# Seven block products in all four feed-forwards of a two-layer flow-matching trunk

## The chip, the cores and the metric

One core of one Trainium2 chip runs the whole program. The metric is device time in microseconds (us), from the launch to the end of the program; lower is better. Engines are called TensorE (PE in the profile, PEld its weight loads), VectorE (DVE), ScalarE (ACT), GpSimd (POOL) and SyncE (SP, which issues the loads).

## The reference, cut to what matters

```python
def swiglu(h, w_gu, w_down):
    g, u = jnp.split(h @ w_gu, 2, axis=-1)
    return (jax.nn.silu(g) * u) @ w_down

def run_layer(x, cond, lp, rope, ctx):
    mod = (jax.nn.silu(cond) @ lp['w_mod'] + lp['b_mod']).reshape(cond.shape[0], N_MOD, 1, D_MODEL)
    nw = lp['norm_w']
    h = rmsnorm(x, nw[0]) * (1 + mod[:, 1]) + mod[:, 0]
    x = x + 0.5 * mod[:, 2] * swiglu(h, lp['ffn1_wgu'], lp['ffn1_wd'])
    h = rmsnorm(x, nw[1]) * (1 + mod[:, 4]) + mod[:, 3]
    out, new_ctx = token_mix(h, lp, rope, ctx)
    x = x + mod[:, 5] * out
    h = rmsnorm(x, nw[2]) * (1 + mod[:, 7]) + mod[:, 6]
    x = x + 0.5 * mod[:, 8] * swiglu(h, lp['ffn2_wgu'], lp['ffn2_wd'])
    return x, new_ctx
```

Two layers; 128 context and 512 latent tokens; model width 1024; feed-forward width 2816; all in float32. The nine modulation vectors of a layer are nine times eight columns of 128, each a product of two conditioning vectors with a 1024 by 128 block of `w_mod`.

## The kernel before, in words

Activations stand transposed: 8 tiles of 128 features by 640 tokens, in two halves of 320 tokens (`HO = (1, 0)`; half p = 1 goes first, half q = 0 holds the context tokens and so has two segments). Every matrix product is made of three matmuls for each 128 by 128 weight block: weight and activation are each split into a rounded part and a remainder (`wh`, `wl` and `xh`, `xl`), and the three leading products are added up in PSUM. A weight tile of four blocks (128 x 512) is loaded (`w`), copied rounded by ScalarE (`wh`, line 162) and subtracted by VectorE (`wl`, line 171). There are 7 buffers each of `wh` and `wl`, and 3 of `w`.

A feed-forward has 22 blocks f of 128 hidden features. The plain one, `ffn` (line 427), makes for each block and token half 8 x 2 x 3 = 48 matmuls for gate and up, in two halves of 11 blocks, each followed by its part of the down product. `ffn7` (line 483) is used for the last feed-forward alone. It makes 2 blocks plainly (`PLAIN`), and from there each block by seven products of quarter size instead of eight: P1, P2, Q3 to Q7, each 4 x 3 = 12 matmuls, so 84 a block instead of 96. For that, sums of weight quarters are needed (four additions of 128 x 512 on GpSimd a block, `load` and `r1`), sums of activation quarters (once, `sums7` on GpSimd and `split7`), and the results are put together by nine VectorE operations of 128 x 320 a block. Blocks go in chunks of 4, each chunk followed by its down product, 16 groups of 12 matmuls.

In `ffn7` the order is written out by hand: `order` is the list of TensorE's groups, and `put(t, ...)` hangs every other operation on a place t in it. Up to the last chunk everything is kept in program order on its engine (`s.pin`). Each weight tile is split a few places before its group: 5 for most, 3 for Q4.

The modulation columns of later steps are made on VectorE by two multiplications with a running sum, of 128 x 1024 each (`mod_cols`, line 321), from a 512 KB load on SyncE's queue. `mod_steps` (line 348) hands them out along the plain feed-forwards: 56 columns beside the first one of layer 0, 24 and 48 beside the next two (`MOD2`, `STEPS1` to `STEPS3`). The last feed-forward has none. `norm_half` (line 398) and `norm7_half` (line 471) make the normalised input of a half as soon as the half's last sum of squares is there; the last `TAIL` = 2 outputs of the feed-forward before are done half p first, so that p's normalisation can go on beside q's rest.

Of the kernel before, what the change touches and what calls it, by code (L numbers as in the profile page):

```python
# [47 lines left out]
def spread(n, a, b):  # L48

    return lambda i: (min(max(i + 1 - a, 0), b - a) * n) // (b - a) - (min(max(i - a, 0), b - a) * n) // (b - a)  # L50

MOD2 = 3

STEPS1, STEPS2, STEPS3 = (4, 66), (10, 66), (4, 66)

HEAD, TAIL, TAIL_O = 2, 2, 3
# [7 lines left out]
PLAIN, K2 = 2, KT // 2  # L66
# [38 lines left out]
class Trunk:  # L105
# [168 lines left out]
    def start(s, mc):  # L274
# [16 lines left out]
        s.h = [s.H() for _ in range(KT)]  # L291
        bm, nw = mc["sp"][:, S_OFF["bmod"][0]:S_OFF["bmod"][1]], mc["sp"][:, S_OFF["nw"][0]:S_OFF["nw"][1]]
        for f0 in range(0, KT, 4):
            fs = slice(f0, f0 + 4)
            for j in (1, 0):
# [6 lines left out]
                row = s.slots.alloc(512, False, "B")  # L302
# [13 lines left out]
            for h in HO:  # L316
                for f in range(f0, f0 + 4):
                    s.norm_tile(0, h, f, rs[h])

    def mod_cols(s, mc, j, f, pin=False):  # L320

        nc = s.nc
        l, m = mc["l"], mc["m"]
        cs = s.cs
        q = j * KT + f
        w = s.wm[q % 2]
        nc.sync.dma_start(out=w, in_=s.a["wmod"][l, q])
# [20 lines left out]
    def mod_steps(s, n):  # L348

        for _ in range(n):  # L350
            if s.todo:
                mc, j, f = s.todo.pop(0)
                s.mod_cols(mc, j, f, True)
                if f == KT - 1:
                    s.mod_fin(mc, j)
# [71 lines left out]
    def ffn(s, wgu, wd, i, mods, done):  # L427

        step = 0
        for hf in range(2):  # L430
            acts = [s.A(2 * T, True) for _ in range(NH)]
            w = {} if hf else {0: s.ahead}
            for mi, h in s.halves(NH, 0 if hf else HEAD, 0):
                m = hf * NH + mi
                if mi not in w:
                    w[mi] = [s.prep(wgu[m, n], KT) for n in range(2)]
                wg, wu = w[mi]
                av = acts[mi].v(2, r=True)
                sl = s.hs(h)
                g = s.proj(wg, h)  # L440
                u = s.proj(wu, h, ps=s.bank())
                t = s.norm.tile([P, H], F32, name="th", tag="tmp", bufs=4)
                s.act(t, g[:, :H], AF.Tanh, scale=0.5)
                s.stt(t, t, 1.0, g[:, :H], ALU.add, ALU.mult)
                s.tt(t, t, u[:, :H], ALU.mult)
                s.split(av[:, 0, sl], av[:, 1, sl], t)
                s.mod_steps(mods(step))
                step += 1
            if hf == 1:
                s.free(s.h)  # L450
            w = {}
            for o, h in s.halves(KT, 0, TAIL if hf else 0):
                if o not in w:
                    w[o] = s.prep(wd[o][:, hf * NH:hf * NH + NH, :], NH)
                sl = s.hs(h)
                ps = s.bank() if (2 * o + h) % 2 else s.wbank()
                s.mms(ps[:, :H], w[o], s.hl_of(acts, sl), NH)
                s.x_update(ps, i, o, h)
                if hf == 1:
                    done(o, h)  # L460
                s.mod_steps(mods(step))
                step += 1
            for a in acts:
                a.free()
# [5 lines left out]


    def norm7_half(s, i, h):

        p, q = HO
        if h == p:
            s.h = [s.H() for _ in range(KT)]
            s.xf = [s.slots.alloc(2 * H, False, "B").v(2) for _ in range(K2)]
        else:
            reg = [s.A(4 * H).v(2, 2) for _ in range(K2 // 2)]
            s.xq = [reg[k // 2][:, k % 2] for k in range(K2)]  # L480
        ps = s.bank()
        s.mm(ps[:, :H], s.ones, s.ss[h])
        r = s.norm_r(ps)
        for k in range(KT):
            t = s.norm_tile(i, h, k, r)
            f = (s.xf if h == p else s.xq)[k % K2][:, k // K2]
            for c, a, b in s.segs(h):
                o = slice(a - h * H, b - h * H)
                s.act(f[:, o], t[:, o], AF.Identity, bias=s.mB[:, c, i, k:k + 1])
# [31 lines left out]
    def ffn7(s, wgu, wd, i, mods, done):  # L521
        p, q = HO
        step = [0]

        def beside():
            s.mod_steps(mods(step[0]))
            step[0] += 1


        sums = [s.A(4 * H, True).v(2, 2, r=True) for _ in range(3 * K2 // 2)]  # L530
        s.s7 = [[sums[(3 * k + j) // 2][:, (3 * k + j) % 2] for j in range(3)] for k in range(K2)]
        acts = [s.A(2 * T, True) for _ in range(PLAIN)]
        w = {0: s.ahead}
        n = 0
        for mi, h in s.halves(PLAIN, PLAIN, 0):
            if mi not in w:
                w[mi] = [s.prep(wgu[mi, e], KT) for e in range(2)]
            g = s.proj(w[mi][0], h)
            u = s.proj(w[mi][1], h, ps=s.bank())
            av, sl = acts[mi].v(2, r=True), s.hs(h)  # L540
            t = s.norm.tile([P, H], F32, name="th", tag="tmp", bufs=4)
            s.act(t, g[:, :H], AF.Tanh, scale=0.5)
            s.stt(t, t, 1.0, g[:, :H], ALU.add, ALU.mult)
            s.tt(t, t, u[:, :H], ALU.mult)
            s.split(av[:, 0, sl], av[:, 1, sl], t)
            if h == q:
                s.sums7(n)
                n += 1
            beside()
        w = {}  # L550
        per = WK // PLAIN
        for o in range(KT):
            if o % per == 0:
                r, (wh, wl) = s.raw(), s.hilo()
                for e in range(per):
                    s.nc.sync.dma_start(out=r[:, e * PLAIN:e * PLAIN + PLAIN, :], in_=wd[o + e][:, :PLAIN, :])
                s.split(wh, wl, r)
            for h in (q, p):
                ps = s.bank() if (2 * o + h) % 2 else s.wbank()
                xs = s.hl_of(acts, s.hs(h))  # L560
                for k in range(PLAIN):
                    e = o % per * PLAIN + k
                    s.three(ps[:, :H], (wh[:, e, :], wl[:, e, :]), xs(k), k == 0, k == PLAIN - 1)
                s.x_update(ps, i, o, h)
                beside()
            if o < K2:
                if n < K2:
                    s.sums7(n)
                    n += 1
# [7 lines left out]
        order, chunks = [], []
        m = PLAIN
        while m < NM:
            chunks.append(range(m, min(m + WK, NM)))  # L580
            m += WK
        tails = set()
        for ci, ch in enumerate(chunks):
            for f in ch:
                new = [(f, n) for n in ("P1", "Q5", "P2", "Q6", "Q3", "Q7")]
                if f > PLAIN:
                    done3 = f == ch[0]
                    new = [x for x in new if not (done3 and x[1] in ("P1", "Q5", "P2"))]
                    if not done3:
                        new.insert(1, (f - 1, "Q4"))  # L590
                order += new
# [3 lines left out]
            if ci + 1 < len(chunks):  # L595
                g = f + 1
                order += [(g, "P1"), (f, "Q4"), (g, "Q5"), (g, "P2")]
# [26 lines left out]
        def tile(f, n, src):  # L624

            def fn():
                ws[f, n] = s.hilo()
                s.split(*ws[f, n], src())
            return fn

        for f in range(PLAIN, NM):
# [36 lines left out]
            put(Q7 + 2, lambda d=d, f=f: s.stt(d["q"], d["q"], 1.0, prods[f, "c"], ALU.add, ALU.mult))  # L668
            put(Q7 + 2, lambda d=d: s.stt(d["q"], d["q"], -1.0, d["t5"], ALU.mult, ALU.mult))
# [6 lines left out]
            put(Q7 + 3, lambda d=d, f=f: s.act(out(f, q)[:, 0], d["q"]))  # L676
            put(Q7 + 4, lambda d=d, f=f: s.tt(out(f, q)[:, 1], d["q"], out(f, q)[:, 0].bitcast(F32), ALU.subtract))
# [1082 lines left out]
```

## Time and profile before

| | us |
|---|---|
| median of 3 runs | 3153.7 (3150.43 to 3154.25) |
| the profiled execution's own time | 3150.53 |
| its span, first to last instruction | 3148.7 |
| TensorE busy | 3087.9 |
| VectorE busy | 2136.4 |
| ScalarE busy | 1220.8 |
| GpSimd busy | 140.0 |

Busy time is the time in which an engine had at least one of its instructions under way. Instructions of one engine overlap in the profile at their ends, so what a series of them takes is read from start to start. A window of the profile is a stretch in us from the span's start. The feed-forwards lie at about 56 to 533, 1142 to 1611, 1612 to 2090 and 2708 to 3149 us; the rest is the start and the two mixers.

### The profile page before, as it was taken

To read this page: it belongs to the slowest core of one execution; us is meant where nothing else is said; L and a number is where in the kernel's file an instruction comes from. 1 tells how busy PE (TensorE), PEld (TensorE's weight loads), DVE (VectorE), ACT (ScalarE), POOL (GpSimd) and SP (SyncE) were. 2 spreads that over 40 slices of the span, in tenths; PEclk is the share of its full clock that TensorE was granted. 3 is DMA by queue.
4 is the path that set the end of the run, shared out by engine and by line. 5 is a ranking of instruction groups with operands and counts; after the bars stand their busy time and mean duration, and the time that the engine had idled before them with its cause. 6 is when DMAs were issued, how large, how long until landed. Compare 5 with 4: busy or idle time off the path is not lost.

```text
span 3148.7 us, 54263 instructions
## 1 busy us (share of the span) xinstructions
PE 3087.9 (98%) x21206; PEld 2929.5 (93%) x21206; DVE 2136.4 (68%) x4268; ACT 1220.8 (39%) x2444; POOL 140.0 (4%) x118
## 2 busy tenths in 40 slices
PE   8999999999999999999999999999999999899999
PEld 5999998998887999999999999989989779799999
DVE  5667677757758774555566666676685687887776
ACT  4222223346544442222242223243464454444443
POOL 0000000000000000000000000000000000232221
PEclk9999999999999999999999999999999999999999
DMA  6445452454322422332323443434533224122222
GB/s 221 135 142 172 140 162 88 138 159 121 120 71 72 142 82 91 115 117 98 115 77 131 148 147 129 146 102 130 167 111 97 65 73 143 54 84 81 83 82 81
DMA packets 261468, 364.87 MB, mean 116 GB/s; under 512 B 97708, under 2 KB 143612, under 8 KB 260476
## 3 DMA queue, kind: packets, MB, share of 16 engines
q1 hardware_dynamic: 252572, 340.66, 34.1%
q10 hardware_dynamic: 8640, 20.76, 1.8%
q8 instruction: 166, 2.72, 0.4%
q14 instruction: 90, 0.74, 0.1%
HBM read 325.37 MB, written 35.96 MB: 115 GB/s over the span
## 4 chain that ended last, share of the span: by engine, by line
PE 89%; DVE 6%; ACT 3%; DMA 1%; issue 1%; SPq 0%; POOL 0%; DVEq 0%; ACTq 0%; POOLq 0%
PE wacc L188 47%; PE acc L188 42%; DVE tn L179 1%; ACT t_A L162 1%; DVE wl L171 1%; DVE t_H L179 1%; DVE t_S L1291 1%; DVE t_A L171 1%; ACT t_H L162 1%; ACT t_B L162 0%; DVE t_A L179 0%; ACT t_W L162 0%; DVE t L179 0%; ACT wh L162 0%; DMA w<-in_wd 0%
## 5 line engine op out<-in xcount | busy, mean ns | idle before, releaser
L188 PE MATMUL wacc<-t_H,wh 128*128 128x320 f32 x5248 | 1188.3, 312 | 24.5 <-ACT t_H L162 9.4
L188 PEld LDWEIGHTS wacc<-t_H,wh 128*128 128x128 f32 x5248 | 877.9, 187 | 52.5 <-DVE t_H L179 14.3
L188 PE MATMUL wacc<-t_H,wl 128*128 128x320 f32 x2624 | 812.3, 311 | 2.5 <-DVE wl L171 2.5
L162 ACT ACTIVATE wh<-w 128x512 fp32r<-128x512 f32 (+2 forms) x772 | 470.4, 613 | 746.5 <-PE wacc L188 488.3
L171 DVE TENSOR_TENSOR wl<-w,wh 128x512 fp32r<-128x512 f32 (+2 forms) x772 | 528.4, 686 | 251.0 <-ACT wh L162 245.1
L188 PE MATMUL acc<-t_H,wh 128*128 128x320 f32 x2496 | 556.6, 308 | 0.0
L188 PE MATMUL acc<-t_A,wh 128*128 128x320 f32 x2272 | 503.6, 308 | 0.2 <-DVE t_A L171 0.2
L188 PEld LDWEIGHTS wacc<-t_H,wl 128*128 128x128 f32 x2624 | 491.5, 187 | 10.3 <-issue 5.3
L188 PE MATMUL wacc<-t_A,wh 128*128 128x320 f32 x2048 | 468.2, 310 | 9.3 <-DVE tg L179 5.5
L188 PEld LDWEIGHTS acc<-t_H,wh 128*128 128x128 f32 x2496 | 418.5, 188 | 0.8 <-ACT wh L162 0.2
L188 PE MATMUL acc<-t_H,wl 128*128 128x320 f32 x1248 | 383.6, 308 | 0.0
L188 PEld LDWEIGHTS acc<-t_A,wh 128*128 128x128 f32 x2272 | 380.1, 188 | 0.8 <-DVE t_A L171 0.5
L188 PEld LDWEIGHTS wacc<-t_A,wh 128*128 128x128 f32 x2048 | 345.2, 188 | 17.3 <-DVE tg L179 6.6
L188 PE MATMUL acc<-t_A,wl 128*128 128x320 f32 x1136 | 350.0, 308 | 0.3 <-DVE wl L171 0.3
L188 PE MATMUL wacc<-t_A,wl 128*128 128x320 f32 x1024 | 317.3, 310 | 2.0 <-DVE wl L171 2.0
L188 PEld LDWEIGHTS acc<-t_H,wl 128*128 128x128 f32 x1248 | 234.0, 188 | 0.1
L188 PEld LDWEIGHTS acc<-t_A,wl 128*128 128x128 f32 x1136 | 213.3, 188 | 0.5 <-DVE wl L171 0.5
L179 DVE SCALAR_TENSOR_TENSOR t_A<-acc,mG,t_A 128x320 f32<-128x320 f32 (+1 forms) x192 | 88.4, 479 | 178.8 <-PE acc L188 173.7
L188 PEld LDWEIGHTS wacc<-t_A,wl 128*128 128x128 f32 x1024 | 192.5, 188 | 5.2 <-DVE wl L171 2.2
L171 DVE TENSOR_TENSOR th<-th,acc 128x320 f32<-128x320 f32 x136 | 66.0, 487 | 186.9 <-PE acc L188 186.9
L162 ACT ACTIVATE t_A<-th 128x320 fp32r<-128x320 f32 x176 | 82.7, 471 | 248.4 <-DVE th L171 221.6
L179 DVE SCALAR_TENSOR_TENSOR t_W<-t_W 128x1024 f32<-128x1024 f32 x128 | 156.3, 1221 | 2.1
(201 smaller groups left out, 3086.0 us busy)
## 6 DMA issues: line engine op xcount, KB each, us to landing
w<-in_wgu SPq DMA_DIRECT2D x292, 256.0 KB, 2.8
t_W<-in_wmod SPq DMA_DIRECT2D x128, 512.0 KB, 4.1
w<-in_win SPq DMA_DIRECT2D x168, 256.0 KB, 3.0
w<-in_wd SPq DMA_DIRECT2D x136, 256.0 KB, 2.8
gd<-tg SPq DMA_DIRECT2D x96, 160.0 KB, 2.2
tg<-gd SPq DMA_DIRECT2D x96, 160.0 KB, 2.3
t_B<-in_wgu SPq DMA_DIRECT2D x40, 256.0 KB, 2.8
w<-in_wd SPq DMA_DIRECT2D x48, 192.0 KB, 2.4
```

The lines of the kernel that those rows point to most:

```text
L162: return s.order(s.nc.scalar.activation(out=out, in_=in_, func=func, **kw))
L171: return s.order(s.nc.vector.tensor_tensor(out=out, in0=a, in1=b, op=op))
L179: return s.order(s.nc.vector.scalar_tensor_tensor(out=out, in0=a, scalar=sc, in1=b, op0=op0, op1=op1, **kw))
L188: return s.order(s.nc.tensor.matmul(out, lhsT, rhs, start=start, stop=stop, **kw))
L1291: nc.vector.tensor_reduce(out=nm2.ap[:, i:i + 1], in_=ps[:, :H], axis=AX.X, op=ALU.max)
```

## The change

All four feed-forwards go through `ffn7`, with four settings (`CHUNKS`): the sizes of the chunks, how many blocks after the first chunk are still plain (`then`), and how many modulation columns go with each step of the first chunk's gate and up, and of its down product. The first chunk is plain: 6 blocks, then 2 more, in the first feed-forwards of both layers (8 plain, 14 by seven products), and 3 blocks in the second ones (3 plain, 19 by seven products). `MOD2` goes from 3 to 4, so 32 columns belong to the second feed-forward and 40 to the third. Columns left over after the first chunk are spread evenly over the places of `order`. The seven products of a block come in the order P1, Q5, Q6, P2, Q7, Q3 (Q4 after the next block's P1), and what reads PSUM at a place is put ahead of the modulation, and both ahead of the splits of weights. In the normalisation the extra copies of half p are done later (`later`), and half q is copied first and split from the copy. `ffn` and the separate schedule of columns go.

```diff
-MOD2 = 3
-STEPS1, STEPS2, STEPS3 = (4, 66), (10, 66), (4, 66)
-HEAD, TAIL, TAIL_O = 2, 2, 3
+MOD2 = 4
+TAIL, TAIL_O = 2, 3
-PLAIN, K2 = 2, KT // 2
+CHUNKS = (((6, 4, 4, 4, 4), 2, 1, 0.5), ((3, 4, 4, 4, 3, 4), 0, 0, 0.25), ((6, 4, 4, 4, 4), 2, 1, 0.5), ((3, 4, 4, 4, 3, 4), 0, 0, 0))
+K2 = KT // 2
...
+    def mod_next(s, n):
+        s.owed += n
+        while s.owed >= 1 and s.todo:
+            s.owed -= 1
+            mc, j, f = s.todo.pop(0)
+            load, a, b = s.mod_cols(mc, j, f)
+            load()
+            s.pin = True
+            a()
+            s.pin = False
+            b()
...
+    def norm7_tile(s, i, h, k, r):
+        x, hv = s.x[k], s.h[k].v(2, r=True)[:, :, s.hs(h)]
+        if h == HO[0]:
+            t = s.xf[k % K2][:, k // K2]
+            A, B = s.mA[:, 1, i, k:k + 1], s.mB[:, 1, i, k:k + 1]
+            s.stt(t, x[:, s.hs(h)], A, r, ALU.mult, ALU.mult)
+            s.act(hv[:, 0], t, AF.Identity, bias=B)
+            s.stt(hv[:, 1], t, B, hv[:, 0].bitcast(F32), ALU.add, ALU.subtract)
+            s.later.append(lambda: s.act(t, t, AF.Identity, bias=B))
+            return
...
+        s.split(hv[:, 0], hv[:, 1], t)
...
+        acts[0] = s.A(2 * T, True)
+        todo = [s.later[:K2], s.later[K2:]] + [[lambda k=k: s.sums7(k)] for k in range(K2)]
+        if not then:
+            sums()
+            todo += [[lambda k=k: s.split7(k)] for k in range(K2)]
+        s.first = True
 
         def beside():
-            s.mod_steps(mods(step[0]))
-            step[0] += 1
...
+            if not s.first:
+                s.mod_next(mods)
+            s.first = False
+            if todo:
+                for fn in todo.pop(0):
+                    fn()
+        eight(0, n0, beside)
+        w0 = {}
         for o in range(KT):
...
+            w0[o] = s.prep(wd[o][:, :n0, :], n0)
             for h in (q, p):
                 ps = s.bank() if (2 * o + h) % 2 else s.wbank()
...
+                s.mms(ps[:, :H], w0[o], s.hl_of([acts[f] for f in range(n0)], s.hs(h)), n0)
                 s.x_update(ps, i, o, h)
...
+                s.mod_next(dmods)
...
+        if then:
+            sums()
+            todo += [[lambda k=k: s.split7(k)] for k in range(K2)]
+            eight(n0, then, lambda: [fn() for fn in todo.pop(0)])
+        rest()
...
+        n, end = len(s.todo), min(tails) - 8
+        for e, (mc, j, f) in enumerate(s.todo):
+            t = e * end // n
+            for fn, d in zip(s.mod_cols(mc, j, f), (0, 4, 5)):
+                put(t + d, fn, late=1)
...
-            s.ffn(s.a["wgu1"][l], s.a["wd1"][l], 0, spread(len(s.todo), *(STEPS3 if l else STEPS1)), s.normed(1, s.ahead_mix(l)))
+            s.ffn7(s.a["wgu1"][l], s.a["wd1"][l], 0, CHUNKS[2 * l], s.normed(1, s.ahead_mix(l)))
...
-                s.ffn(s.a["wgu2"][l], s.a["wd2"][l], 2, spread(len(s.todo), *STEPS2), done)
+                s.ffn7(s.a["wgu2"][l], s.a["wd2"][l], 2, CHUNKS[2 * l + 1], done)
```

## Rows read from the trace of the kernel before

**Rows 1.** The page: part 1, busy time by engine; part 4, chain by engine.
```profile
PE 3087.9 (98%) x21206; PEld 2929.5 (93%) x21206; DVE 2136.4 (68%) x4268; ACT 1220.8 (39%) x2444; POOL 140.0 (4%) x118
...
PE 89%; DVE 6%; ACT 3%; DMA 1%; issue 1%; SPq 0%; POOL 0%; DVEq 0%; ACTq 0%; POOLq 0%
```

**Rows 2.** Windows view (columns in its first line): a stretch of plain feed-forward.
```profile
core 0: us, PE busy (x) PEld busy (x) DVE busy (x) ACT busy (x) POOL busy (x), PEclk, DMA share, GB/s
258.00:410.00 152.00, 152.00 (x1038) 152.00 (x1038) 105.41 (x199) 41.91 (x78) 0.00 (x0) 1.00 0.44 147
```

**Rows 3.** Windows view: one chunk of the last feed-forward, four blocks and down product.
```profile
2917.63:2929.95 12.32, 12.32 (x86) 12.32 (x86) 8.64 (x14) 6.34 (x13) 4.08 (x3) 1.00 0.25 86
2929.95:2942.27 12.32, 12.32 (x86) 12.32 (x86) 11.25 (x17) 6.48 (x14) 5.22 (x5) 1.00 0.25 84
2942.27:2954.60 12.33, 12.33 (x86) 12.33 (x86) 11.57 (x17) 6.55 (x15) 5.55 (x5) 1.00 0.21 67
2954.60:2966.90 12.30, 12.30 (x86) 12.30 (x85) 8.60 (x15) 5.82 (x13) 1.78 (x2) 1.00 0.23 65
2966.90:2995.10 28.20, 28.20 (x194) 28.20 (x194) 18.59 (x38) 6.65 (x11) 5.50 (x4) 1.00 0.30 94
```

**Rows 4.** Timeline, VectorE, third feed-forward: the two multiplications of a modulation column.
```profile
1659.85 1.22 DVE L179 SCALAR_TENSOR_TENSOR t_C<-t_W 128x1024 f32<-128x1024 f32 x1
...
1660.99 0.69 DVE L171 TENSOR_TENSOR wl<-w,wh 128x512 fp32r<-128x512 f32 x1
1661.59 1.22 DVE L179 SCALAR_TENSOR_TENSOR t_W<-t_W 128x1024 f32<-128x1024 f32 x1
...
1662.74 0.69 DVE L171 TENSOR_TENSOR wl<-w,wh 128x512 fp32r<-128x512 f32 x1
```

**Rows 5.** Timeline, GpSimd and VectorE, last feed-forward: one block's four weight sums.
```profile
2871.67 1.31 POOL L165 TENSOR_TENSOR w<-t_B 128x512 f32<-128x512 f32 x1 [4.29 <-DMA t_B<-in_wgu]
2871.79 1.54 DVE L179 SCALAR_TENSOR_TENSOR th<-th,tg 128x320 f32<-128x320 f32 x1
2873.06 1.42 POOL L165 TENSOR_TENSOR t_B<-t_B,w 128x512 f32<-128x512 f32 x1
2873.25 1.77 DVE L171 TENSOR_TENSOR wl<-t_B,wh 128x512 fp32r<-128x512 f32 x1
2876.17 1.41 POOL L165 TENSOR_TENSOR w<-w 128x512 f32<-128x512 f32 x1 [1.69 <-DVE wl L171]
2876.81 1.32 DVE L171 TENSOR_TENSOR wl<-t_A,wh 128x512 fp32r<-128x512 f32 x1 [0.38 <-ACT wh L162]
2878.26 1.42 POOL L165 TENSOR_TENSOR t_A<-t_A,w 128x512 f32<-128x512 f32 x1 [0.68 <-POOL w L165]
2878.46 0.48 DVE L171 TENSOR_TENSOR acc<-tg,acc 128x320 f32<-128x320 f32 x1
2878.86 1.37 DVE L171 TENSOR_TENSOR wl<-w,wh 128x512 fp32r<-128x512 f32 x1
```

**Rows 6.** Timeline, last feed-forward: Q4's split on VectorE, Q4's first matmuls on TensorE.
```profile
2868.07 0.69 DVE L171 TENSOR_TENSOR wl<-t_B,wh 128x512 fp32r<-128x512 f32 x1
...
2871.83 0.45 PE L188 MATMUL wacc<-t_A,wh 128*128 128x320 f32 x2
```

**Rows 7.** Windows view: the beginning of the last feed-forward.
```profile
2710.00:2800.00 90.00, 78.21 (x488) 74.61 (x487) 84.40 (x137) 45.47 (x107) 42.19 (x35) 0.94 0.20 68
```

**Rows 8.** Waits of TensorE (us, times, longest) from 2700 to 2800.
```profile
PE wacc L188 <- DVE t_H L179: 5.7, 5, 2.3
PE wacc L188 <- DVE wl L171: 2.9, 2, 2.0
```

**Rows 9.** Timeline: first feed-forward's last output of p; mixer's first matmuls.
```profile
507.93 0.55 DVE L179 SCALAR_TENSOR_TENSOR t_A<-acc,mG,t_A 128x320 f32<-128x320 f32 x1 [3.20 <-PE acc L188]
...
518.30 0.49 PE L188 MATMUL wacc<-t_H,wh 128*16 128x320 f32 x2
...
533.58 0.62 PE L188 MATMUL wacc<-t_H,wh 128*16 128x320 f32 x3 [3.21 <-ACT t_H L162]
```

More of the change, by code (lines that the diff above doesn't have):

```diff
@@ L290, in start @@
         rs = [s.norm_r(ps) for ps in pss]
-        s.h = [s.H() for _ in range(KT)]
+        for h in HO:
+            s.norm7_begin(h)
         bm, nw = mc["sp"][:, S_OFF["bmod"][0]:S_OFF["bmod"][1]], mc["sp"][:, S_OFF["nw"][0]:S_OFF["nw"][1]]
@@ L346, in mod_fin @@
                 s.ts(mc["G"][:, c, i, :], mc["G"][:, c, i, :], 0.5 if i == 1 else 0.25, ALU.mult)
[L348 to L355, printed above, removed]
+    def mod_next(s, n):
[9 more added lines that the diff above has]
+            b()
+            if f == KT - 1:
+                s.mod_fin(mc, j)
     def mod_ctx(s):
@@ L425, in halves, with norm7_begin @@
         return o + [(t, a) for t in range(n - last, n)] + [(t, b) for t in range(n - last, n)]
[L427 to L475, printed above, removed]
+    def norm7_begin(s, h):
+        if h == HO[0]:
             s.h = [s.H() for _ in range(KT)]
             s.xf = [s.slots.alloc(2 * H, False, "B").v(2) for _ in range(K2)]
+            s.later = []
         else:
@@ L519, in three @@
         s.mm(ps, wl, xh, False, last, skip_group_check=True)
-    def ffn7(s, wgu, wd, i, mods, done):
-        p, q = HO
-        step = [0]
-        def beside():
-            s.mod_steps(mods(step[0]))
-            step[0] += 1
[L530 to L551, printed above, removed]
-        for o in range(KT):
[L553 to L557, printed above, removed]
@@ L577, in ffn7 @@
[L577 to L581, printed above, removed]
+                s.mod_next(dmods)
+                if todo:
+                    for fn in todo.pop(0):
+                        fn()
+        if then:
[3 more added lines that the diff above has]
+        rest()
+        order = []
         tails = set()
+        begun = set()
@@ L583, in ffn7 @@
         for ci, ch in enumerate(chunks):
+            if ci == 0:
+                continue
             for f in ch:
[L585 to L590, printed above, removed]
+                if f < plain:
+                    continue
+                new = [(f, n) for n in ("P1", "Q5", "Q6", "P2", "Q7", "Q3")]
+                if f in begun:
+                    new = new[4:]
+                elif f > plain:
+                    new.insert(1, (f - 1, "Q4"))
@@ L596, in ffn7 @@
                 g = f + 1
-                order += [(g, "P1"), (f, "Q4"), (g, "Q5"), (g, "P2")]
+                begun.add(g)
+                order += [(g, "P1")] + [(f, "Q4")] * (f >= plain) + [(g, "Q5"), (g, "Q6"), (g, "P2")]
                 order += [(ci, o, h, 0, K) for o, h in os]
@@ L627, in fn @@
                 ws[f, n] = s.hilo()
-                s.split(*ws[f, n], src())
+                m = len(chunks[f]) if type(n) is int else WK
+                wh, wl = ws[f, n]
+                s.split(wh[:, :m], wl[:, :m], src()[:, :m])
             return fn
-        for f in range(PLAIN, NM):
+        for f in range(plain, NM):
             P1, Q5, P2, Q6, Q3, Q7, Q4 = [pos[f, n] for n in ("P1", "Q5", "P2", "Q6", "Q3", "Q7", "Q4")]
```

125 lines of the change are left out of this document (70 added, 55 removed).

## The prediction

> **What bounds the kernel now.** I read the page first: TensorE is busy 98% of the span and 89% of the chain that ended last [rows 1]. Then windows of plain feed-forward: 1038 matmuls in 152.00 us, no idle time, the clock whole [rows 2]: one matmul of 320 tokens each 0.1464 us, so 12 take 1.76. So matmuls that go are time saved, wherever the other engines keep up. Whether they do is read in the one stretch that already works by seven products, the last feed-forward: windows of one chunk, block by block [rows 3]. TensorE is full there too, but VectorE is busy 8.6, 11.3, 11.6 and 8.6 us in the four blocks of 12.3, and 18.6 of 28.2 in the down product. Nothing but weight splits and assembly is in that; modulation runs beside none of it. So the bound after the change has to be looked for in VectorE's second and third block of each chunk, where 1.07 and 0.76 us are free.
>
> I call the four feed-forwards A, B (layer 0), C, D (layer 1).
>
> **Matmuls.** A block by seven products has 84 instead of 96. By `CHUNKS`, 14 blocks of A and C and 19 of B change: 14 x 12 + 19 x 12 + 14 x 12 = 564 fewer. D has 19 such blocks instead of 20: 12 more. 552 x 0.1464 = 81 us saved, certain as far as TensorE is fed.
>
> **Modulation columns.** What I count in the code differs from the change's words. There are 56, 32 and 40 columns in A, B, C. Beside the first chunk go 11 + 8 = 19 in A and in C (one for each gate-and-up step but the first, one for every other down group) and 4 in B. So 42 of 128 lie there, and 37, 28 and 21 are spread over the places of the block products. A and C have about 137 such places, B 188. A block is 7 places, a down product 16: A gets 37 x 7 / 137 = 1.89 columns a block and 4.3 a down product; B and C 1.05 and 2.4. A column is two multiplications, each 1.14 us from its start to the next instruction's [rows 4], so 2.28: in A 4.3 us more VectorE work a block and 9.8 a down product, in B and C 2.4 and 5.5.
>
> **The wait for GpSimd.** In the block products GpSimd makes four weight sums a block, and the trace shows what that does to VectorE [rows 5]. The `th<-th,tg` begun at 2871.79 takes 1.54 us, where an operation of its size takes 0.48, and it ends 0.35 after GpSimd's sum. Three splits begun beside a sum take 1.77, 1.32 and 1.37 instead of 0.69 [rows 4]. The excess is 1.06 + 1.08 + 0.63 + 0.68 = 3.4 us a block; it is within the 11.6 of [rows 3]. `acc<-tg,acc`, which reads PSUM, passes beside a sum in 0.48. A modulation multiplication has both inputs in SBUF, like those that wait, so a fuller VectorE waits longer for the same sums. The sums of such a block are 1.31 + 1.42 + 1.41 + 1.42 = 5.6 us; 2.2 are not yet waited for. Bounds for the addition: nothing, or four fifths of 2.2 = 1.7 a block, since six of VectorE's sixteen operations a block, 2.4 of its 12 us, read PSUM and pass. I take 0.6 in A and 0.4 in B and C, nearer to the trace's own share, because sums are released by splits and so begin where VectorE often has a PSUM operation or a wait next.
>
> **What TensorE loses by it.** I carry the lag of VectorE's queue through a chunk, block by block: work added less time free [rows 3], never below zero. What lag is borne is read at Q4, whose split has the shortest lead: it ends at 2868.76, and Q4 starts at 2871.83 [rows 6], so 3.1 us, or 2.0 where a multiplication of 1.14 comes in front.
> A: 4.9 a block against 3.68, 1.07, 0.76, 3.70 free: +1.2, +3.8, +4.1, +1.2 = 10.4; its down product gets 9.8 + 0.8 against 9.6 free, +1.0. The lag is never recovered, so a whole chunk costs 11.4. Two blocks (2.4 + 1.0), two chunks (22.8), and a last one whose end has no columns (about 9) are 35, less 2.8 borne: 32 us.
> B and C: 2.8 a block: 0, +1.7, +2.0, -0.9: a peak of 3.7 against 2.0 to 3.1 borne, so 0.6 to 1.7 a chunk, say 1.2, and the down product (5.9 against 9.6) takes the rest away. 8.5 chunks: 10 us.
> Together 42. With nothing added to the waits: 4.3 a block in A gives 8.2 a chunk, 22 in all; B and C peak at 3.0, 4 in all: 26. With 1.7 added: A 16.5 a chunk, 50; B and C 4.6 a chunk, 39: 89.
>
> **Beginnings.** D now begins so: in 90 us, 488 matmuls, which need 71.4: 18.6 lost, VectorE busy 84.4 [rows 7], and TensorE waits for q's normalised tiles and splits [rows 8]. After, D has three plain blocks instead of two: 14 us of gate and up and 7 of down products more, against some 6 of VectorE work; the waits for q stay. I take half of the 18.6 back: -9. B begins the same way with 4 columns (9 us) in 21 us of down product: what is left of 18.6, and half of the columns: +13. C has six plain blocks before anything has to be ready, but the same q half at the start: +6. A starts with both halves nearly ready: +2. Sum +12, from 0 to +25.
>
> **Ends.** The last two outputs of q cover p's normalisation. In A that chain runs from 507.93 to 518.30, 10.4 us [rows 9], under two groups of 33 matmuls, 9.7. In the change these are 12 matmuls each, 3.5. So 5 to 6 us open in A, B and C. Before mixers q's wait of 3.21 [rows 9] shrinks to about 1.5, since q's chain starts earlier too. Sum +13, bounds 8 and 18.
>
> **At nothing.** The columns in the first chunk of A and C: a step there is 7.0 us of TensorE against 2.28 for a column, 1.2 of splits and 1.2 of assembly; if that cover failed the beginnings' +25 holds it. The loads of the columns on SyncE's queue: the two buffers are refilled every 3.7 places (6.5 us) in A, and a load waits for the multiplication two columns back; weight loads stand behind it, but with 8 places (14 us) of lead. If VectorE lags by more than that lead allows, this adds to the case below.
>
> **Sum.** 3150.5 - 81 + 42 + 12 + 13 = 3136.5 for the profiled execution, which is 3.2 below the median of 3153.7. I forecast 3138.
>
> **Rivals.**
> *VectorE's lock with GpSimd decides (slower).* Every two-input operation waits a sum out, 1.7 more a block. For it: the four waits of [rows 5], each to the end of the sum. Against: of 5.6 us only 3.4 were waited for. It turns the sign from about 1.1 added: 3150.5 - 81 + 89 + 12 + 13 = 3184. Chance 0.24. The Trainium skill, SBUF — State Buffer, section "SBUF: two separate sides", says that VectorE (with two SBUF inputs) and GpSimd share a port pair as an exclusive lock, held for the whole instruction, and the other blocks fully. By that rule this rival is the upper end of the sum, 3184; the ends of the waits in [rows 5] agree with it.
> *Lags and edges are covered (faster).* Q4's lead is not what binds; other splits are earlier, so B and C lose nothing and A 27, and beginnings and ends stay at 4 and 8: 3150.5 - 81 + 39 = 3108. For it: in B and C the whole chunk's work, 58.7 + 4 x 2.8 + 5.9 = 76, fits in 77.5. Chance 0.18.
> *Edges cost more (no change).* Both at their upper ends, 25 and 18: 3155 against the median's 3153.7. For it: [rows 7], where VectorE was full. Chance 0.08.
> *The columns do run mostly beside the first chunk,* as the change's words say: no lag, 3150.5 - 81 + 25 = 3095. The code speaks against it, and kept order rules out that the columns move. Chance 0.04.
>
> **Numbers.** The forecast's own case (3120 to 3153) has 0.46. A measurement can tell about 0.2%, 6.3 us. Faster: 0.40 of the forecast, 0.18, 0.04: 0.62. Same: 0.04 of the forecast, 0.06 of the edges, 0.02 of the lock: 0.12. Slower: 0.22 of the lock, 0.02 of the edges, 0.02 of the forecast: 0.26. The range takes in the bounds, from 3098 (below the covered case) to 3188 (above the lock's).
>
> **What would show it.** Right: 552 matmuls fewer; in A's block products VectorE at 95% or more and TensorE idle for some 30 us, waiting for `wl` and for operations on tg and th; in B and C a few us a chunk in the third block; multiplications of 1.22 us drawn out to above 2 beside a sum; gaps of 5 us at the ends of A, B and C; D's first 90 us with fewer gaps. Wrong: TensorE full in A's block products (the lag was borne), or idle by more than 10% in B and C (the lock, or loads behind the columns), or large gaps at the beginnings.

## The result, and the profile after

The changed kernel takes 3183.8 us in the median (3182.5 to 3188.0) against 3152.8 for the kernel before: a ratio of 1.0099 (95% interval 1.0087 to 1.0112). It is 1% slower, where 3138 and "faster" were forecast; the time that came is the 3184 of the rival in which VectorE's lock with GpSimd decides. The profiled execution took 3188.0, its span 3185.9.

First the page of the changed kernel: busy time by engine, and the chain that ended last by engine. They answer to [rows 1].

```profile
PE 3038.6 (95%) x20654; PEld 2864.4 (90%) x20654; DVE 2515.7 (79%) x4804; ACT 1356.3 (43%) x2812; POOL 465.9 (15%) x350
...
PE 37%; DVE 6%; ACT 2%; issue 1%; DMA 1%; SPq 0%; POOL 0%; DVEq 0%; ACTq 0%; POOLq 0%
```

21206 - 20654 = 552 matmuls went, as counted. VectorE gained 379 us and GpSimd 326. TensorE has a smaller share of a longer span, so the time has to be looked for in TensorE's gaps. The two traces are laid side by side at fixed marks: behind A, B and C the first matmul that reads the normalised half p, and ahead of B and D the last matmul of half p's sum of squares. A has the start with it. The stretches of the profiled executions, in us:

| | A | mixer 0 | B | C | mixer 1 | D | span |
|---|---|---|---|---|---|---|---|
| before | 518.3 | 608.6 | 478.5 | 469.1 | 608.6 | 465.6 | 3148.7 |
| after | 544.9 | 605.9 | 491.5 | 480.6 | 610.2 | 452.8 | 3185.9 |
| without columns beside block products | 506.8 | 606.3 | 464.3 | 462.7 | 608.0 | 455.1 | 3103.2 |

The third row is the first experiment below. It splits the difference: up to it lies what the block products and their edges bring, and from it to "after" what the columns beside them cost.

The windows view of the changed kernel, in order: a chunk of C block by block with its down product, a whole chunk of A (its down product first), and the third block and the down product of a chunk of D, which has no columns. Columns as in [rows 2]; the answers to [rows 3] are the last two.

```profile
1874.40:1886.70 12.30, 12.30 (x85) 12.07 (x83) 12.18 (x18) 4.61 (x10) 5.24 (x4) 1.00 0.41 129
1886.70:1899.00 12.30, 11.70 (x80) 11.66 (x80) 11.98 (x16) 4.91 (x11) 5.49 (x4) 1.00 0.39 128
1899.00:1914.60 15.60, 13.47 (x91) 12.98 (x89) 15.16 (x24) 6.49 (x15) 6.25 (x4) 1.00 0.23 86
1914.60:1930.50 15.90, 13.97 (x85) 13.94 (x85) 13.64 (x24) 8.50 (x19) 2.79 (x2) 0.89 0.31 100
1930.50:1958.90 28.40, 28.40 (x196) 28.40 (x195) 23.86 (x46) 6.64 (x12) 4.75 (x3) 1.00 0.42 139
...
341.00:430.10 89.10, 78.89 (x530) 77.41 (x529) 87.13 (x144) 29.87 (x63) 23.70 (x16) 1.00 0.41 138
...
2923.70:2936.00 12.30, 12.30 (x86) 12.30 (x85) 10.66 (x17) 6.59 (x14) 5.69 (x5) 1.00 0.19 65
2948.30:2976.55 28.25, 28.25 (x195) 28.25 (x194) 17.59 (x36) 6.54 (x11) 5.49 (x4) 1.00 0.26 85
```

The four blocks of C take 56.1 us where 49.2 are free of loss, though VectorE's work in blocks and down product, 76.8, would fit in 77.45. VectorE is full in the blocks (53.0 of 56.1) and has 4.5 us to spare in the down product, too late. In A VectorE is full throughout.

How a stall comes about is read in one block of that chunk, on the timeline of the changed kernel (start, duration, engine, line; in brackets the idle time before and what ended it):

```profile
1893.23 1.22 DVE L174 SCALAR_TENSOR_TENSOR t_C<-t_W 128x1024 f32<-128x1024 f32 x1
1894.20 1.42 POOL L160 TENSOR_TENSOR w<-t_B 128x512 f32<-128x512 f32 x1 [4.36 <-DMA t_B<-in_wgu]
1894.37 1.79 DVE L166 TENSOR_TENSOR wl<-t_B,wh 128x512 fp32r<-128x512 f32 x1
...
1895.69 1.62 POOL L160 TENSOR_TENSOR t_B<-t_B,w 128x512 f32<-128x512 f32 x1
1896.09 2.31 DVE L174 SCALAR_TENSOR_TENSOR t_W<-t_W 128x1024 f32<-128x1024 f32 x1
...
1899.84 0.48 DVE L174 SCALAR_TENSOR_TENSOR th<-th,wacc 128x320 f32<-128x320 f32 x1
...
1899.96 0.87 ACT L157 ACTIVATE t_A<-th 128x320 fp32r<-128x320 f32 x2 [5.20 <-DVE th L174]
...
1901.57 0.43 ACT L157 ACTIVATE tg<-wacc 128x320 f32<-128x320 f32 x1
...
1902.05 0.55 PE L183 MATMUL wacc<-t_H,wh 128*128 128x320 f32 x2 [2.12 <-ACT tg L157]
```

The second multiplication of a column takes 2.31 us beside GpSimd's sum, where the first took 1.22, and a split 1.79 instead of 0.69. VectorE's `th<-th,wacc` then comes 5.2 us behind the end of Q4, whose result it reads; in the same block of a chunk of C without columns (the first experiment) it comes 1.5 behind. ScalarE waits 5.2 us for it with its next instruction, an output copy. Behind that stands the copy of Q6's PSUM (`tg<-wacc`), and Q7 waits 2.12 us for that. VectorE was 3.7 late, and TensorE bore 1.6 of it. The same kernel's waits of TensorE in all of C's block products (us, times, longest) are of this kind and of one other, where VectorE itself is last:

```profile
PE wacc L183 <- ACT tg L157: 7.5, 6, 2.1
PE wacc L183 <- DVE tg L166: 6.2, 6, 2.5
```

### The profile page after: what moved, and what is told of

Read it like the earlier page. It is cut to its first block, busy times and chain, and to the rows that moved or that the text cites. A ratio compares the mean times of both kernels' runs of the same rounds, so it can differ in the third digit from the quotient of the medians.

```text
span 3185.9 us, 54589 instructions
## 1 busy us (share of the span) xinstructions
PE 3038.6 (95%) x20654; PEld 2864.4 (90%) x20654; DVE 2515.7 (79%) x4804; ACT 1356.3 (43%) x2812; POOL 465.9 (15%) x350
## 5 line engine op out<-in xcount | busy, mean ns | idle before, releaser
L183 PE MATMUL wacc<-t_H,wh 128*128 128x320 f32 x4512 | 1036.3, 314 | 61.6 <-ACT tg L157 34.6
L183 PEld LDWEIGHTS wacc<-t_H,wh 128*128 128x128 f32 x4512 | 758.7, 188 | 97.6 <-ACT tg L157 42.0
L183 PE MATMUL acc<-t_A,wh 128*128 128x320 f32 x3440 | 762.8, 308 | 1.4 <-ACT t_A L157 1.4
L183 PE MATMUL wacc<-t_H,wl 128*128 128x320 f32 (+1 forms) x2256 | 703.8, 313 | 2.6 <-DVE wl L166 2.6
L183 PEld LDWEIGHTS acc<-t_A,wh 128*128 128x128 f32 x3440 | 576.8, 188 | 2.2 <-ACT t_A L157 1.6
L183 PE MATMUL acc<-t_A,wl 128*128 128x320 f32 x1720 | 530.4, 308 | 3.9 <-DVE wl L166 3.9
L183 PEld LDWEIGHTS wacc<-t_H,wl 128*128 128x128 f32 (+1 forms) x2256 | 424.8, 188 | 9.1 <-issue 4.0
L183 PE MATMUL acc<-t_H,wh 128*128 128x320 f32 x1760 | 401.0, 312 | 0.1
L174 DVE SCALAR_TENSOR_TENSOR t_A<-acc,mG,t_A 128x128 f32<-128x128 f32 (+1 forms) x480 | 200.7, 445 | 123.1 <-PE acc L183 113.4
L166 DVE TENSOR_TENSOR wl<-t_A,wh 128x512 fp32r<-128x512 f32 x132 | 148.8, 1127 | 36.9 <-ACT wh L157 36.9
```

What stands on the lines that cost most here:

```text
L166: return s.order(s.nc.vector.tensor_tensor(out=out, in0=a, in1=b, op=op))
L174: return s.order(s.nc.vector.scalar_tensor_tensor(out=out, in0=a, scalar=sc, in1=b, op0=op0, op1=op1, **kw))
L183: return s.order(s.nc.tensor.matmul(out, lhsT, rhs, start=start, stop=stop, **kw))
```

## The experiments

All totals are medians, and all stretches, lines and views come from the profiled execution; in every group of runs the kernel before took 3152.0 to 3154.5. "Theory" stands, in each, for what was held by then.

**1. Without the columns beside block products.** In `ffn7` the leftover columns' two multiplications read 8 of 1024 inputs, so their products are mostly left out; their loads stay (`short` is `mod_cols` with `[:, :8]` on the multiplications' operands).

```diff
-            for fn, d in zip(s.mod_cols(mc, j, f), (0, 4, 5)):
+            for fn, d in zip(short(mc, j, f), (0, 4, 5)):
```

> Leaves out most of the modulation columns that lie beside block products: both multiplications over 8 of 1024 inputs, loads kept. In the changed kernel's trace TensorE loses about 42 us in A's block products, 27 in B's and 25 in C's. Theory (VectorE's added work, columns and waits for sums together): all of it goes, 3184 - 94 = 3090 (3080 to 3105). Rival (loads of columns ahead of weight loads, or the beginnings and ends alone): less than 30 us goes, 3155 or more.

**2. Without GpSimd's weight sums,** all columns kept: the splits read unsummed tiles.

```diff
-                s.add(r["X"], r["U1"], r["U2"])
+                r["X"] = r["U1"]
...
-            put(a + 1, lambda r=r: s.add(r["U1"], r["U1"], r["G1"]))
-            put(a + 2, lambda r=r: s.add(r["G1"], r["X"], r["G1"]))
-            put(a + 3, lambda r=r: s.add(r["G2"], r["G2"], r["G1"]))
```

> Leaves out the four weight sums of each block on GpSimd (raw quarters are split in their place); all columns stay. Theory (the lock): a block is 8.2 us of VectorE without waits, with 4.3 of columns 12.5 against 12.3 of TensorE in A, 10.6 in B and C: nearly all of the 94 us goes, 3090 to 3105. Rival (columns alone fill VectorE, the waits matter little): 3150 or more.

Measured: 3103.2 without columns (ratio 0.984) and 3091.0 without sums (0.980). The windows view of a whole chunk: C without columns; C, then A, without sums.

```profile
1857.40:1934.80 77.40, 77.40 (x530) 77.40 (x529) 59.67 (x129) 31.76 (x64) 22.95 (x16) 1.00 0.40 130
```

```profile
1845.40:1922.80 77.40, 77.40 (x529) 77.40 (x529) 63.60 (x129) 32.19 (x64) 0.00 (x0) 1.00 0.39 130
319.30:396.70 77.40, 77.40 (x529) 77.40 (x529) 73.06 (x147) 31.58 (x64) 0.00 (x0) 1.00 0.50 164
```

TensorE is full in all three. Sums alone cost the chunks nothing, and neither do columns alone, not even A's 12 a chunk. Both together cost 83 us (38.1 in A, 27.2 in B, 17.9 in C, from the table). The loads run in both kernels, so they are not it. The second edit also frees the splits from waiting for their sums, but that is not where the time went: in whole chunks of A, B and C of the changed kernel TensorE waits for `tg`, never for `wl`, and VectorE hardly idles (3.1 of 56.1 us in C's blocks, 2.0 of 89.1 in A's chunk). Without columns, what is left against the kernel before is the edges: the four stretches of feed-forward change by -11.5, -14.2, -6.4, -10.5, their matmuls by -24.6, -33.4, -24.6, +1.8, so the edges are +13, +19, +18 and -12, together 38.

**3. ScalarE's order.** The output copies, which wait for `th`, go behind the PSUM copies (`e` is 1; half p's copy and the remainders move likewise). The theory was that ScalarE's order makes the stall.

```diff
-            put(Q3 + 4, lambda d=d, f=f: s.act(out(f, q)[:, 0], d["q"]))
+            put(Q3 + 4 + e, lambda d=d, f=f: s.act(out(f, q)[:, 0], d["q"]), late=e)
```

> Moves the output of a block (ScalarE's rounding of q and p, VectorE's remainders) one place later, behind ScalarE's copy of the running product that TensorE waits for before Q7. Theory (VectorE's lag is borne for less than its queue allows, because ScalarE, kept in order, waits for VectorE's product before it makes that copy): B and C lose half of their 52 us less, 3150 to 3165. Rival (VectorE is simply full): within 5 us of 3184, the waits move to Q4.

Measured: 3181.6 (1.009). TensorE's waits over C's blocks in this kernel:

```profile
PE wacc L183 <- DVE tg L166: 11.0, 8, 3.7
PE wacc L183 <- ACT tg L157: 2.1, 2, 1.2
```

Now TensorE waits for VectorE directly, at Q4: ScalarE's order only chose where VectorE's lag was met. This theory fell.

**4. The old order of the products** (P1, Q5, P2, Q6, Q3, Q7), with its places for the assembly.

```diff
-                new = [(f, n) for n in ("P1", "Q5", "Q6", "P2", "Q7", "Q3")]
+                new = [(f, n) for n in ("P1", "Q5", "P2", "Q6", "Q3", "Q7")]
```

> Undoes one part of the change: the seven products in the order of the kernel before (P1, Q5, P2, Q6, Q3, Q7), with its places for the assembly and for Q6's split. Theory (ScalarE's copy behind the output): the output lies three places ahead of the copy again, 3155 to 3175, unless Q4, now one group behind Q7, takes over. Rival (VectorE is full whatever the order): within 5 us of 3184.

Measured: 3191.5 (1.012). The new order is not the cause; the old one is no better.

**5. Two columns a step beside the first chunk,** so that fewer are left for the block products.

```diff
-CHUNKS = (((6, 4, 4, 4, 4), 2, 1, 0.5), ((3, 4, 4, 4, 3, 4), 0, 0, 0.25), ((6, 4, 4, 4, 4), 2, 1, 0.5), ((3, 4, 4, 4, 3, 4), 0, 0, 0))
+CHUNKS = (((6, 4, 4, 4, 4), 2, 2, 0.5), ((3, 4, 4, 4, 3, 4), 0, 0, 0.25), ((6, 4, 4, 4, 4), 2, 2, 0.5), ((3, 4, 4, 4, 3, 4), 0, 0, 0))
```

> Two columns instead of one with each gate-and-up step of the first chunk in A and C, so 30 lie there; 26 stay beside A's block products and 10 beside C's, B keeps 28. The first chunk has 7.06 us a step against 4.6 of columns and 2.4 of other VectorE work: full. Theory (columns and waits for sums together overfill VectorE in the blocks): per chunk A loses 5 to 7 instead of 12, C 0 to 1 instead of 6, so 3184 - 20 - 22 = 3142 (3130 to 3155), B unchanged. Rival (the first chunk was full already): what is won is lost there, 3175 or more.

Measured: 3174.8 (1.0066). A's whole chunks, taken from one down product to the next, go from 91.1 and 89.1 to 83.6 and 85.6, C's from 84.4 and 82.9 to 79.4 and 79.0 (free: 77.45), a little less than expected. But the cover that the prediction priced at nothing is gone. The windows view of C's first chunk and its down product with two columns a step:

```profile
1640.00:1725.00 85.00, 78.07 (x503) 75.10 (x502) 83.25 (x154) 28.89 (x65) 16.49 (x16) 0.98 0.47 154
```

VectorE is full there, and C takes 10.4 us more than in the changed kernel up to the end of its first down product, A 4.7. One column a step is about what the first chunk holds.

**6. A plain, with 96 columns;** B and D by block products without columns, C with its first chunk's 1.5 a step and three quarters a down group.

```diff
-CHUNKS = (((6, 4, 4, 4, 4), 2, 1, 0.5), ((3, 4, 4, 4, 3, 4), 0, 0, 0.25), ((6, 4, 4, 4, 4), 2, 1, 0.5), ((3, 4, 4, 4, 3, 4), 0, 0, 0))
+CHUNKS = (((6, 4, 4, 4, 4), 2, 1, 0.5), ((3, 4, 4, 4, 3, 4), 0, 0, 0), ((6, 4, 4, 4, 4), 2, 1.5, 0.75), ((3, 4, 4, 4, 3, 4), 0, 0, 0))
...
-            s.ffn7(s.a["wgu1"][l], s.a["wd1"][l], 0, CHUNKS[2 * l], s.normed(1, s.ahead_mix(l)))
+            if l == 0:
+                s.ffn(s.a["wgu1"][l], s.a["wd1"][l], 0, lambda i: at(i + 1) - at(i), s.normed(1, s.ahead_mix(l)))
```

> A goes back to the plain feed-forward and takes 96 columns, 40 of them of layer 1; B has none, C 28 of its 32 beside its first chunk, 4 beside blocks. Theory: B, C and D run as without columns (3103 in that run), A's 168 matmuls come back (25 us) and its edges go: 3125 (3110 to 3140), faster than both kernels' 3152 and 3184. Rival (96 columns overfill VectorE in the plain feed-forward, 197 + 219 us of 473 by the trace of before): 3150 or more.

Measured: 3132.3 (0.993, interval 0.991 to 0.995). B takes 456.5 (before 478.5). C takes 469.6 against 469.1: its edges and the first chunk's columns eat the 24.6 of its matmuls. A takes 8 more: TensorE is full up to 500 us and then waits up to 2.7 for `wl`; 96 columns are a little too many for one plain feed-forward.

**7. Four outputs done p first at the ends** instead of two, so that p's normalisation has more cover.

```diff
-TAIL, TAIL_O = 2, 3
+TAIL, TAIL_O = 4, 3
```

> Four instead of two outputs of the last chunk are done half p first (TAIL = 4), so q's rest is four groups of 12 matmuls, 7.0 us instead of 3.5. Theory (the gap of 5.3 us at the ends of A, B and C is p's normalisation, uncovered): three gaps shrink by 3.5, 3184 - 10 = 3174 (3170 to 3178). Rival (VectorE is late there because of its queue): 3180 or more.

Measured: 3190.1 (1.0116); missed. TensorE's gaps for p and q at the end of A, in the changed kernel and in this one:

```profile
544.91 1.25 PE L183 MATMUL wacc<-t_H,wh 128*16 128x320 f32 x4 [5.32 <-ACT t_H L157]
...
559.18 1.01 PE L183 MATMUL wacc<-t_H,wh 128*16 128x320 f32 x4 [1.16 <-ACT t_H L157]
```

```profile
539.37 0.91 PE L183 MATMUL wacc<-t_H,wh 128*16 128x320 f32 x3 [2.47 <-ACT t_H L157]
...
556.39 1.14 PE L183 MATMUL wacc<-t_H,wh 128*16 128x320 f32 x3 [3.94 <-ACT t_H L157]
```

What p gains (2.9) q loses (2.8), as its last outputs now stand behind more of p's. A, B and C become 3 to 6 us shorter, but the two mixers 10 and 4 longer. In them the granted clock stands at 1.2 GHz for 24 and 20 us instead of 11 and 10. At that level the trace has a matmul every 0.267 us instead of 0.147, so this is worth about 6 and 4 us; most of the rest of the first is q's gap. Why the clock fell more often isn't shown.

**8. Columns by the blocks' room,** most of them beside the first and last block of a chunk and the down product (`cum` is a running sum of 0.6, 0.53 or 0.13 a place).

```diff
-            t = e * end // n
+            t = int(np.searchsorted(cum, cum[-1] * (e + 0.5) / n)) - 4
```

> The leftover columns are not spread evenly over the places but by the room that VectorE has in the kernel before: weight 0.6 at a place of a down product, 0.53 in the first and last seven places of a chunk's blocks, 0.13 between. Theory (VectorE's queue, with the room read block by block: 18.8 us a chunk, 8.2 columns): B (6.6 a chunk) and C (6.8) lose under 1 us a chunk, 3184 - 45 = 3139, and A (11.8) loses 8 instead of 12, so 3115 to 3145. Rival (what counts is the sum over a chunk, or every wait for a sum): 3165 or more.

Measured: 3168.9 (1.0045): A gains 2.8 us, B 10.1, C 6.8, about a third of what was expected. Of the multiplications beside B's and C's block products 27 of 87 now meet a sum, instead of 37 of 83, and still a whole chunk loses 2.0 to 5.3 us. The first block, which had room without columns, is full with them (VectorE 12.27 of its 12.3 us in a chunk of C). Room read block by block was not enough; why no more was won isn't shown.

**9. Block products in B and D only,** with no column beside any: A plain with 80 columns, C plain with 48. **10. Block products in D only,** with the change's order and beginning; of the two edits shown 9 has the first alone, and in both `ffn` is the plain one.

```diff
-            s.ffn7(s.a["wgu1"][l], s.a["wd1"][l], 0, CHUNKS[2 * l], s.normed(1, s.ahead_mix(l)))
+            s.ffn(s.a["wgu1"][l], s.a["wd1"][l], 0, lambda i, n=n: at(i + 1, n) - at(i, n), s.normed(1, s.ahead_mix(l)))
...
-                s.ffn7(s.a["wgu2"][l], s.a["wd2"][l], 2, CHUNKS[2 * l + 1], done)
+                s.ffn(s.a["wgu2"][l], s.a["wd2"][l], 2, lambda i: 0, done)
```

> Block products in B and D alone, three blocks plain each and no columns beside them; A and C are plain feed-forwards, A with 80 columns, C with 48. Theory: B keeps what it has in the run with A plain (436 us against 469 before, -33), D what it has in the changed kernel (-12), A and C run as before: 3153 - 45 = 3108 (3100 to 3118). Rival (edges, or A with 80 columns, give it back): 3125 or more.

> Only D's part of the change (three blocks plain instead of two, the new order of products, copies later), and the columns as 80 and 48 beside plain A and C, none beside plain B. Theory (fewer waits at D's beginning, as in the changed kernel's trace): 3153 - 12 = 3141 (3137 to 3146). Rival (columns in A cost): 3150 or more.

Measured: 3125.0 (0.9908, interval 0.9892 to 0.9925) and 3142.9 (0.9966, 0.9953 to 0.9979). The first beats both kernels, by less than expected; the second is as expected. A chunk of B in the ninth, and one in the changed kernel, in the windows view:

```profile
1270.20:1347.60 77.40, 77.40 (x530) 77.40 (x529) 55.99 (x97) 31.68 (x64) 22.84 (x16) 1.00 0.27 82
```

```profile
1302.50:1385.20 82.70, 79.48 (x530) 78.96 (x529) 73.44 (x122) 30.36 (x64) 23.49 (x16) 0.98 0.36 122
```

B's chunks are free of loss, yet B gains 21.1 us and not the 33.4 of its matmuls: the edges. The mixers take 4.8 and 6.4 more than before. In each of them the granted clock stands at 1.2 GHz for 20.5 us instead of 10.2, worth about 4 and 3 us of that. The block products aren't the cause: the mixer of layer 1 is the same code in both runs and takes 615.0 in the ninth and 608.9 in the tenth. D alone gains 12.8 us.

**11. Half sums:** each weight sum over half of its tile, all columns kept; one of the four edits is shown (the products' weights are wrong sums; the rest is computed).

```diff
-            put(a + 1, lambda r=r: s.add(r["U1"], r["U1"], r["G1"]))
+            put(a + 1, lambda r=r: s.add(r["U1"][:, :2], r["U1"][:, :2], r["G1"][:, :2]))
```

> The changed kernel with GpSimd's weight sums over half of each tile, so the other half stays raw; all columns stay. Theory (VectorE waits each sum out: 3.3 to 3.6 us a block): the waits halve, A loses about 6 a chunk instead of 12, B and C 0 to 1 instead of 5 to 6: 3115 to 3130. Rival (a wait has a fixed cost whatever the sum's size): 3170 or more.

Measured: 3105.3 (0.985), better than expected. A chunk of C and one of A:

```profile
1860.20:1937.70 77.50, 77.50 (x531) 77.50 (x530) 68.50 (x129) 31.32 (x65) 15.31 (x16) 1.00 0.39 130
324.90:405.60 80.70, 78.54 (x529) 77.36 (x529) 78.18 (x144) 29.83 (x63) 15.07 (x16) 1.00 0.47 152
```

B and C lose nothing and A 3 to 5 us a chunk. The waits inside VectorE's operations with two SBUF inputs (their durations less those they have when no sum runs), over whole chunks, are 1.5, 1.2 and 1.4 us a block in A, B and C, where the changed kernel has 3.9, 3.3 and 3.7. A single wait shrinks too: the second multiplication of a column takes at most 1.77 us, where the changed kernel has up to 2.33 (1.22 without a sum). So the waits go by the length of the sums; a fixed price for each meeting of the two engines would have stayed.

**12. B's and C's multiplications hung on places Q3, P1 and the down product,** meant to be clear of sums. **13. One place earlier** (Q7 and the down product), which by the twelfth run's trace would meet fewer.

```diff
+        clear, used = [t for t in range(4, end + 4) if len(order[t]) == 5 or order[t][1] in ("Q3", "P1")], -2
...
+                used = min((x for x in clear if x >= used + 2), key=lambda x: abs(x - 4 - t))
+                t = used - 4
```

> In B and C alone, the same number of columns at nearly the same density, but each column's two multiplications stand where a block's weight sums are not running (at Q3 and the next P1, or in a down product) instead of anywhere; A as in the changed kernel. Theory (the term that was set too small is the waiting added when a multiplication and a sum meet): VectorE's waits in B and C fall from 3.3 us a block to 2.5 or less, a chunk loses 1 to 3 instead of 5 to 6, 3184 - 27 = 3157 (3148 to 3166). Rival (the middle blocks are overfilled whatever the place): 3174 or more.

> As the run before, but the two multiplications one place earlier, at Q7 and Q3: in that run the second one met the first sum of the next block, which starts with its loads and not with a place (a sum from 1895.94, the multiplication from 1895.98 to 1898.33). Theory (waits with the sums are what was set too small): VectorE's waits in B and C fall from 3.3 to 3.5 us a block to about 2.4, and a chunk loses 2 to 4 instead of 5 to 6: 3184 - 20 = 3164 (3154 to 3172). Rival (the middle blocks are overfilled by the columns' own 2.4 us, waits or not): 3176 or more.

Measured: 3182.4 (1.0091) and 3172.8 (1.0057, interval 1.004 to 1.0074). In 12 the aim was missed, as its timeline shows:

```profile
1895.94 1.31 POOL L160 TENSOR_TENSOR w<-t_B 128x512 f32<-128x512 f32 x1 [5.09 <-DMA t_B<-in_wgu]
1895.98 2.35 DVE L174 SCALAR_TENSOR_TENSOR t_W<-t_W 128x1024 f32<-128x1024 f32 x1
...
1897.34 2.15 POOL L160 TENSOR_TENSOR t_B<-t_B,w 128x512 f32<-128x512 f32 x1
```

This sum, the block's first, started when its load had landed, not at a place of the order, so placing the multiplications alone doesn't keep them clear. 32 of 86 meet a sum, and VectorE's waits are 3.4 us a block in B and 3.7 in C, as before the edit (3.3 and 3.7). In 13 only 11 of 86 meet one, and B and C become 7.1 and 5.8 us shorter; but the waits are still 3.3 and 3.4, as the splits now wait, and a whole chunk still loses 4.5 to 5.3. Where the multiplications meet the sums decides a small part of the loss; how much lag TensorE can bear in the middle blocks is not settled by it.

## Why the prediction was wrong, point by point

**Matmuls (-81): right.** 552 went, and where nothing waits a chunk of block products takes 77.4.

**VectorE's work in the block products: right.** The forecast was 76 us a chunk in B and C, and 58.7 + 4 x 4.9 + 10.6 = 88.9 in A. Measured: 73.4 to 76.8, and 87.1 to 88.1. On the base that the sum stood on, the kernel before's chunk of [rows 3], whose operations hold waits of 2.8 us a block (the 3.4 was one block of another chunk), the added wait, by whole chunks, is 1.1 in A (taken 0.6) and 0.5 and 0.9 in B and C (taken 0.4), within its bounds. Against the changed kernel's own D, where those waits are 2.2, it is 1.1 to 1.7.

**A (32): nearly right.** 38. Its two whole chunks lost 13.7 and 11.6 against 11.4 forecast, and the last one 10 against 9.

**"What lag is borne" in B and C (10): this step failed.** The columns cost 27.2 + 17.9 = 45 us there, 5.3 to 7.0 a whole chunk instead of 1.2. The carry itself gave a peak of 3.7 us, and VectorE was 3.7 late in the block shown above. But 2.0 to 3.1 of it were to be borne, read at Q4's split, which is made ahead of need. The place that bound was another: the assembly's `th` and `tg`, which have to follow the products at once, and ScalarE's copies queued behind them; 1.6 was borne there. Second, the carry let a lag be lost once. In C's chunk TensorE lost 0.6, 2.1 and 1.9 us in three blocks one after another, 4.6 in all. Third, a spell at half the clock (1.2 GHz of 2.4) followed the last of these. The windows view of the changed kernel, 3 us of C's fourth block:

```profile
1919.40:1922.40 3.00, 3.00 (x16) 3.00 (x16) 3.00 (x7) 1.47 (x3) 0.00 (x0) 0.69 0.30 87
```

TensorE is busy without a gap and gets 16 matmuls through instead of 22; the granted clock has fallen to 1.2 GHz for part of it, after the 1.93 us gap at 1916.57. In the spell of 3.4 us a matmul starts every 0.267 us instead of 0.147, which costs 1.5. Together 6.2 of the chunk's 7.0. With 1.6 borne the carry gives some 2 us a chunk, and the clock's 1.5 came with three gaps in the 8.5 chunks of B and C (the spells from 1358.0, 1525.3 and 1917.8): 2 to 4 us a chunk stay unexplained. A candidate, argued only, is that VectorE idles 3.1 us in these blocks, once visibly for a ScalarE copy that stood behind the stalled one, so its lag feeds on itself.

**The lock rival.** It named the time (3184) and the mechanism: experiments 1, 2 and 11 show that columns and sums cost something only together, and by the sums' length. It priced it by a wait of 1.7 more a block, where 0.5 to 1.1 more were enough, since TensorE bore less. That its 3184 came is partly luck: it is made of 50 in A, 39 in B and C and 25 at the edges, and 38, 45 and 38 came. The Trainium skill, SBUF — State Buffer, section "SBUF: two separate sides", says that a VectorE operation with two SBUF inputs and a GpSimd operation hold their shared port pair for a whole instruction. The timeline agrees: the multiplication beside a sum takes 2.31 instead of 1.22 and ends 1.1 behind the sum's end. How long the waits are together was read from the rows.

**Beginnings (+12): the seams were missed.** D's edges gained 12 to 15 us (its stretch is 10.5 or 12.8 shorter, in spite of 1.8 more of matmuls), where 9 were forecast. The answer to [rows 7], the windows view of the same stretch of D's beginning in the changed kernel, is

```profile
2760.00:2850.00 90.00, 87.42 (x589) 86.47 (x590) 74.19 (x132) 43.55 (x99) 36.75 (x30) 1.00 0.23 77
```

3.8 us are lost where 18.6 were. B's beginning cost the 13 forecast: of 90 us near its start 16.7 are lost in the changed kernel (the first view below), and 3.5 of the same 90 in the kernel before (the second).

```profile
1155.00:1245.00 90.00, 79.52 (x501) 75.63 (x500) 83.44 (x161) 44.03 (x101) 26.55 (x23) 0.96 0.29 98
```

```profile
1131.00:1221.00 90.00, 88.48 (x591) 86.63 (x591) 58.45 (x129) 37.31 (x78) 0.00 (x0) 1.00 0.25 87
```

Not seen was the seam inside A and C, where block products follow plain blocks: some 6 us each, most of it one gap, shown here in the changed kernel on TensorE, after the ScalarE copy behind which its own releaser stands:

```profile
216.92 0.47 ACT L157 ACTIVATE t_A<-th 128x320 fp32r<-128x320 f32 x1 [4.20 <-DVE th L166]
...
217.77 0.74 PE L183 MATMUL wacc<-t_A,wh 128*128 128x320 f32 x2 [4.24 <-ACT tg L157]
```

It is the same coupling, and it is there without columns too, as the first experiment's kernel shows:

```profile
217.30 0.56 PE L183 MATMUL wacc<-t_A,wh 128*128 128x320 f32 x2 [4.24 <-ACT tg L157]
```

The price was looked for where the feed-forwards begin, and it lies where the block products do.

**Ends (+13): about right.** The gap of p at A's end is 5.3 us, as worked out, and q's 1.2 (forecast 1.5). Up to q's first mixer matmul, A's and C's ends cost 4.2 and 4.0 more than before; the seam between B and C, from B's last down product to the end of C's first one, 12.8 more (11 to 12 forecast, as B's end and C's beginning). All edges: 38 where 25 were forecast; the excess is about what the seams inside A and C cost.

**The clock: no term.** Stretches at 1.2 GHz add up to 75 us in the changed kernel, 62 without columns and 31 before (mean granted clock 0.988, 0.990 and 0.995); in the four feed-forwards 54, 40 and 10. By the time that TensorE was busy in them, and by the 0.267 us of a matmul there against 0.147, the clock makes about 10 of the edges' 38 and 7 of the columns' 83. The sum had nothing for it.

**The columns "mostly beside the first chunk".** As counted, they are not: 172 of the 256 multiplications fall behind the plain blocks, beside block products. Experiment 5 shows why more can't go there, and the "at nothing" for one column a step was right.

**The sum with measured terms:** 3148.7 - 81 + 38 (edges) + 83 (columns) - 3 (the mixers, which are 2.3 and 0.6 shorter without the columns) gives 3185.7, the span being 3185.9. Of the error of some 50 us between profiled executions (3188.0 against 3136.5), 35 are the columns in B and C, 13 the edges and 6 A, less the mixers' 3.

## What to carry to other kernels

Work that fits an engine by its sum over a chunk can still stall the one that it feeds: read the longest run of blocks without room, and take the lag that is borne from the operation with the least lead, not from one that is made ahead. Two loads that are each free, a filler on VectorE and sums on GpSimd, should be priced together, by the time that they run at the same moment; if one can run in a stage without the other, put it there, as the ninth experiment does (0.991). A change made of parts with different signs is best tried part by part: D and B alone gain, A and C lose what they save.

## What the runs showed of the hardware that was not expected

The waits of VectorE beside GpSimd go by the length of GpSimd's instruction: sums of 128 x 256 (0.83 to 1.05 us each) instead of 128 x 512 (1.38 to 1.65) took the loss in B and C from 5 to 7 us a chunk to nothing, and the longest wait of a column's second multiplication from 1.12 us to 0.55. GpSimd pays too: its `t_B<-t_B,w` sum takes 1.65 us in the mean in the changed kernel and 1.50 without columns, and 2.15 in the twelfth experiment's block shown above, in which a multiplication had begun first. And of the two gaps of about 2 us on TensorE in the chunk shown, one was followed by some 3.4 us at 1.2 GHz and the other by none; over the whole span there are 18 such spells, of 3.4 to 10 us, where the kernel before has 7. So a stall can cost nearly twice what it lasts.
